# Bulk loads of 16 rows in two buffers in place of 14 rows in three, with the last scaling on GpSimd

## The chip, the core and the metric

The kernel runs on one core of one Trainium2 chip. SyncE issues the transfers and 16 DMA engines carry them; VectorE, ScalarE and GpSimd compute. A load has landed when the last of its 16 engines has reported. The metric is the device time of one execution in microseconds (us). Times given here are medians of several executions on the same chip; the profile describes one execution, and its span (first to last instruction) is about 1.5 us shorter than the device time. The program uses one core, so the "slow" state of a run means only that the run was more than 1.5% above the fastest of the same kernel; the granted clock was 1.0 in all runs.

## The reference

```python
x = np.random.randn(32, 512, 1024).astype(np.float32)
out = (np.sum(x, axis=-1) / 1024.0).astype(np.float32)      # shape (32, 512)
```

There are 16384 rows of 1024 floats, 67 MB to read and 64 KB to write. A "row" in this document means one row on each of the 128 partitions, 0.52 MB; there are 128 of them.

## The kernel before

The first 112 rows come in bulk loads into rotating buffers. VectorE sums each tile with one instruction; of the last tiles, ScalarE sums some rows with its accumulator. Then come ever smaller loads, so that little work is left when the last bytes land. The last two rows are cut up: `row` between ScalarE and VectorE, and the very last one into `pa`, `pb` and `pc`.

```python
main = [(2, 0)] + [(14, 0)] * 6 + [(14, 4), (12, 5)]      # (rows, rows of them on ScalarE)
last = [(8, 4), (4, 2), (2, 1)]
bulk = ctx.enter_context(tc.tile_pool(name="bulk", bufs=3))
...
for rows, on_act in main:
    t = bulk.tile([P, 14, D], F32, name="t")
    load(t[:, :rows, :], x_main[:, j : j + rows, :])       # one DMA, issued from SyncE
    sums(res[:, j : j + rows], t, rows, on_act)            # reduce_sum on VectorE, act_sum on ScalarE
    j += rows
...
c = 768                                                    # row: VectorE sums 768, ScalarE 256
a, b = 448, 704                                            # pa 448 (ScalarE), pb 256 (VectorE), pc 320
...
nc.gpsimd.tensor_scalar_mul(out=res, in0=res, scalar1=scale)
# store of res
act_sum(pc[:, D - b : D - b + 1], pa)
nc.vector.reduce_sum(out=pc[:, D - b + 1 :], in_=pb, axis=AX)
nc.vector.scalar_tensor_tensor(out=fin[:, : L - 1], in0=q[:, : L - 1], scalar=scale,
                               in1=r[:, : L - 1], op0=MULT, op1=ADD)
nc.vector.tensor_scalar(out=scaled, in0=pc, scalar1=scale, scalar2=0.0,
                        op0=MULT, op1=ADD, accum_out=fin[:, L - 1 :])
# store of fin
```

Each partition of a bulk load is one contiguous piece (one descriptor) of 14 * 4 = 56 KB. The load of a tile waits until the tile that had its buffer before has been summed.

## Time and profile before

| | before |
|---|---|
| device time, median | 161.5 us (161.36 to 161.53) |
| span of the profiled run | 159.8 us |
| DMA packets, share of 16 engines' span | 98.0% |
| VectorE busy | 76% |
| landings of 14-row loads | 16.94 us apart |
| VectorE's sum of 14 rows | 15.09 us |
| VectorE idle before each bulk tile | 1.85 us |

The landing distance is the pace of the transfers. The idle time of VectorE before a tile is also a lead: when VectorE frees a buffer, the load in flight lands that much later.

### The profile page before, as it was taken

To read this page: it belongs to the slowest core of one execution; us is meant where nothing else is said; L and a number is where in the kernel's file an instruction comes from. 1 tells how busy PE (TensorE), PEld (TensorE's weight loads), DVE (VectorE), ACT (ScalarE), POOL (GpSimd) and SP (SyncE) were. 2 spreads that over 40 slices of the span, in tenths; PEclk is the share of its full clock that TensorE was granted. 3 is DMA by queue.
4 is the path that set the end of the run, shared out by engine and by line. 5 is a ranking of instruction groups with operands and counts; after the bars stand their busy time and mean duration, and the time that the engine had idled before them with its cause. 6 is when DMAs were issued, how large, how long until landed. Compare 5 with 4: busy or idle time off the path is not lost.

```text
span 159.8 us, 139 instructions
## 1 busy us (share of the span) xinstructions
DVE 121.1 (76%) x17; ACT 19.6 (12%) x37; POOL 0.8 (0%) x6
## 2 busy tenths in 40 slices
DVE  0500059995999599978999599959995996494985
ACT  3000000000000000000000000000001900480973
POOL 0000000000000000000000000000000000001000
DMA  7999999978999999978999999978999999899993
GB/s 250 472 459 459 459 459 459 459 330 359 459 459 459 459 459 459 459 316 373 459 459 459 459 459 459 416 345 388 459 459 427 394 480 505 353 435 390 408 400 132
DMA packets 2592, 67.18 MB, mean 420 GB/s; under 512 B 544, under 2 KB 928, under 8 KB 1056
## 3 DMA queue, kind: packets, MB, share of 16 engines
q1 hardware_dynamic: 2592, 67.18, 98.0%
HBM read 67.11 MB, written 0.07 MB: 420 GB/s over the span
## 4 chain that ended last, share of the span: by engine, by line
DMA 76%; DVE 22%; SPq 1%; issue 0%; DVEq 0%
DMA t<-in_x_dram 56%; DMA row<-in_x_dram 21%; DVE res L153 20%; SPq L142 1%; DVE q L176 1%; DVE scaled L198 0%; DVE pc L193 0%; DVE fin L194 0%; DVEq L198 0%; DVEq L232 0%
## 5 line engine op out<-in xcount | busy, mean ns | idle before, releaser
L153 DVE TENSOR_REDUCE res<-t 128x14 f32<-128x14336 f32 (+3 forms) x9 | 111.2, 12360 | 34.3 <-DMA t<-in_x_dram 34.3
L147 ACT ACTIVATE junk<-t 128x1024 f32<-128x1024 f32 x16 | 16.2, 1013 | 135.9 <-DMA t<-in_x_dram 135.9
L153 DVE TENSOR_REDUCE q<-t 128x4 f32<-128x4096 f32 (+2 forms) x3 | 7.9, 2642 | 2.7 <-DMA t<-in_x_dram 2.5
L147 ACT ACTIVATION_READ_ACCUMULATOR junk<-t 128x1 f32 x16 | 3.0, 187 | 0.0
L147 ACT ACT_TABLE_LOAD x1 | 1.3, 1283 | 1.7 <-PEq L218 1.7
L189 POOL TENSOR_SCALAR res<-res 128x112 f32<-128x112 f32 x1 | 0.5, 494 | 143.8 <-DVE res L153 143.8
L176 DVE TENSOR_REDUCE q<-row 128x1 f32<-128x768 f32 x1 | 1.0, 953 | 0.0
L198 DVE TENSOR_SCALAR_CACHE_REDUCE scaled<-pc 128x322 f32<-128x322 f32 x1 | 0.5, 490 | 0.1
L147 ACT ACTIVATE junk<-pa 128x448 f32<-128x448 f32 x1 | 0.5, 548 | 0.0
L193 DVE TENSOR_REDUCE pc<-pb 128x1 f32<-128x256 f32 x1 | 0.4, 414 | 0.0
L147 ACT ACTIVATE junk<-row 128x256 f32<-128x256 f32 x1 | 0.4, 388 | 0.1
L194 DVE SCALAR_TENSOR_TENSOR fin<-q,r 128x15 f32<-128x15 f32 x1 | 0.2, 176 | 0.0
L147 ACT ACTIVATION_READ_ACCUMULATOR junk<-pa 128x1 f32 x1 | 0.2, 186 | 0.0
L147 ACT ACTIVATION_READ_ACCUMULATOR junk<-row 128x1 f32 x1 | 0.2, 185 | 0.0
L139 POOL MEMSET r<- 128x16 f32 x1 | 0.1, 112 | 1.3 <-POOLq L218 1.3
L218 POOL MEMSET const-bfloat16-1.0<- 128x1 bf16 x1 | 0.1, 103 | 0.0
L218 POOL MEMSET const-uint8-127<- 128x1 uint8 x1 | 0.1, 102 | 0.0
L218 POOL MEMSET const-float32-0.0<- 128x1 f32 x1 | 0.1, 99 | 0.2 <-issue 0.2
L218 POOL MEMSET const-float32-1.0<- 128x1 f32 x1 | 0.1, 99 | 0.0
L198 DVE DVE_READ_ACCUMULATOR scaled<-pc 128x1 f32 x1 | 0.1, 83 | 0.0
## 6 DMA issues: line engine op xcount, KB each, us to landing
t<-in_x_dram SPq DMA_DIRECT2D x7, 7168.0 KB, 35.7
t<-in_x_dram SPq DMA_DIRECT2D x1, 6144.0 KB, 33.3
t<-in_x_dram SPq DMA_DIRECT2D x1, 4096.0 KB, 26.1
t<-in_x_dram SPq DMA_DIRECT2D x2, 1024.0 KB, 18.6
t<-in_x_dram SPq DMA_DIRECT2D x1, 2048.0 KB, 30.5
row<-in_x_dram SPq DMA_DIRECT2D x1, 512.0 KB, 33.2
pa<-in_x_dram SPq DMA_DIRECT2D x1, 224.0 KB, 33.3
pc<-in_x_dram SPq DMA_DIRECT2D x1, 160.0 KB, 33.1
```

The source lines that it names most:

```text
L139: nc.gpsimd.memset(r, 0.0)
L142: tc.keep_in_program_order(nc.sync.dma_start(out=dst, in_=src))
L147: nc.scalar.activation(junk[:, :n], src, COPY, scale=by, accum_out=dst)
L153: nc.vector.reduce_sum(out=dst[:, :d], in_=t[:, :d, :], axis=AX)
L176: nc.vector.reduce_sum(out=q[:, j : j + 1], in_=row[:, :c], axis=AX)
L189: nc.gpsimd.tensor_scalar_mul(out=res, in0=res, scalar1=scale)
L193: nc.vector.reduce_sum(out=pc[:, D - b + 1 :], in_=pb, axis=AX)
L194: nc.vector.scalar_tensor_tensor(out=fin[:, : L - 1], in0=q[:, : L - 1], scalar=scale, in1=r[:, : L - 1], op0=MULT, op1=ADD)
L198: nc.vector.tensor_scalar(out=scaled, in0=pc, scalar1=scale, scalar2=0.0, op0=MULT, op1=ADD, accum_out=fin[:, L - 1 :])
L218: nc = _bacc.Bacc("TRN2", target_bir_lowering=False, num_devices=1)
```

## The change

The intent is fewer and larger loads (64 KB a descriptor, one load fewer), and a shorter tail: the scaling of the last results leaves VectorE for GpSimd, and the splits of the last rows are set anew. To make room, two bulk buffers replace three, and the small tiles get memory of their own.

```diff
-    main = [(2, 0)] + [(14, 0)] * 6 + [(14, 4), (12, 5)]
+    main = [(2, 0)] + [(16, 0)] * 5 + [(16, 2), (14, 6)]
-    bulk = ctx.enter_context(tc.tile_pool(name="bulk", bufs=3))
+    bulk = ctx.enter_context(tc.tile_pool(name="bulk", bufs=2))
-    r = one.tile([P, L], F32, name="r")
-    nc.gpsimd.memset(r, 0.0)
+    r = one.tile([P, 1], F32, name="r")
-        t = bulk.tile([P, 14, D], F32, name="t")
+        if rows > 2:
+            t = bulk.tile([P, 16, D], F32, name="t")
+        else:
+            t = one.tile([P, rows, D], F32, name="t0")
 ... the 8-row tile of the tail moves from bulk to one ...
-    c = 768
+    c = 688
-    a, b = 448, 704
+    a, b = 480, 672
-    nc.vector.scalar_tensor_tensor(
-        out=fin[:, : L - 1], in0=q[:, : L - 1], scalar=scale, in1=r[:, : L - 1], op0=MULT, op1=ADD
+    nc.gpsimd.tensor_scalar_mul(out=fin[:, :j], in0=q[:, :j], scalar1=scale)
+    nc.gpsimd.tensor_scalar(
+        out=fin[:, j : j + 1], in0=q[:, j : j + 1], scalar1=scale, scalar2=r, op0=MULT, op1=ADD
     )
```

More of the change, by code (lines that the diff above doesn't have):

```diff
@@ L162 @@
     for rows, on_act in last:
-        if rows == 8:
-            t = bulk.tile([P, 14, D], F32, name="t")[:, :8, :]
-        else:
-            t = one.tile([P, rows, D], F32, name=f"t{rows}")
+        t = one.tile([P, rows, D], F32, name=f"t{rows}")
         load(t, x_last[:, j : j + rows, :])
@@ L169 @@
         j += rows
-    c = 768
+    c = 688
     row = one.tile([P, D], F32, name="row")
     load(row, x_last[:, j, :])
-    act_sum(r[:, j : j + 1], row[:, c:], by=scale)
+    act_sum(r, row[:, c:], by=scale)
     nc.vector.reduce_sum(out=q[:, j : j + 1], in_=row[:, :c], axis=AX)
-    a, b = 448, 704
+    a, b = 480, 672
     pa = one.tile([P, a], F32, name="pa")
```

## The prediction

> **What bounds the kernel now.** The kernel sums 16384 rows of 1024 floats, 128 rows (0.52 MB) per "row step" of the 128 partitions, and moves 67.18 MB. I read the page's totals first, then the order of time, then short windows over the start, then the last microseconds.
>
> ```profile
> span 159.8 us, 139 instructions
> DVE 121.1 (76%) x17; ACT 19.6 (12%) x37; POOL 0.8 (0%) x6
> ...
> q1 hardware_dynamic: 2592, 67.18, 98.0%
> ```
>
> The packets of the one DMA queue fill 98% of the 16 engines' span; VectorE is busy for 76% only. The chain of waits agrees in kind (DMA 76%, DVE 22%), but its DVE share is misleading: where it walks through a 15.1 us reduction it follows the release of a buffer, and two other loads were in flight at that time. The order of time shows it:
>
> ```profile
> 38.71 15.09 DVE L153 TENSOR_REDUCE res<-t 128x14 f32<-128x14336 f32 x1 [1.87 <-DMA t<-in_x_dram]
> 55.65 15.09 DVE L153 TENSOR_REDUCE res<-t 128x14 f32<-128x14336 f32 x1 [1.84 <-DMA t<-in_x_dram]
> 72.59 15.09 DVE L153 TENSOR_REDUCE res<-t 128x14 f32<-128x14336 f32 x1 [1.86 <-DMA t<-in_x_dram]
> ...
> 123.41 10.82 DVE L153 TENSOR_REDUCE res<-t 128x10 f32<-128x10240 f32 x1 [1.85 <-DMA t<-in_x_dram]
> 137.94 7.62 DVE L153 TENSOR_REDUCE res<-t 128x7 f32<-128x7168 f32 x1 [3.72 <-DMA t<-in_x_dram]
> 147.66 4.42 DVE L153 TENSOR_REDUCE q<-t 128x4 f32<-128x4096 f32 x1 [2.09 <-DMA t<-in_x_dram]
> ```
>
> Columns: start, duration, engine, instruction, then how long the engine sat idle and for whom. Each bulk reduction starts when its load lands, and landings are 16.94 us apart (14 rows), then 14.53 (12 rows, 123.41 to 137.94) and 9.72 (8 rows). That is 1.21 us a row step whatever the load's size: 7.34 MB in 16.94 us is 433 GB/s. From 14 and 12 rows, a row step costs (16.94-14.53)/2 = 1.205 us, and what is left over is 16.94-14*1.205 = 0.07 us per load. So loads carry almost no fixed cost while the queue is full. VectorE finishes each tile 1.85 us before the next lands.
>
> The end, in the order of time:
>
> ```profile
> 156.18 0.39 ACT L147 ACTIVATE junk<-row 128x256 f32<-128x256 f32 x1
> 156.18 0.95 DVE L176 TENSOR_REDUCE q<-row 128x1 f32<-128x768 f32 x1
> 156.72 0.55 ACT L147 ACTIVATE junk<-pa 128x448 f32<-128x448 f32 x1
> 157.17 0.18 DVE L194 SCALAR_TENSOR_TENSOR fin<-q,r 128x15 f32<-128x15 f32 x1
> 157.20 0.19 ACT L147 ACTIVATION_READ_ACCUMULATOR junk<-pa 128x1 f32 x1
> 157.26 0.41 DVE L193 TENSOR_REDUCE pc<-pb 128x1 f32<-128x256 f32 x1
> 157.79 0.49 DVE L198 TENSOR_SCALAR_CACHE_REDUCE scaled<-pc 128x322 f32<-128x322 f32 x1
> 158.31 0.34 SPq L201 DMA_DIRECT2D out_dram<-fin  x1
> ...
> pc<-in_x_dram SPq DMA_DIRECT2D x1, 160.0 KB, 33.1
> ```
>
> The last piece pc is issued at 124.39 and lands 33.1 us later, at 157.49. Its sum starts at 157.79, 0.11 us after VectorE is done with pb at 157.68. So at the very end VectorE, not the transfer, sets the time, by 0.2 to 0.25 us. That is all that the end can give.
>
> **What the Trainium skill says.** "DMA: Bandwidth & Descriptors", section "Where 436 GB/s comes from": the SBUF ports pass 435.2 GB/s. The trace agrees: 433 GB/s between landings. So there is nothing left for larger descriptors to win in mid-stream. The same page, "Latency and other measured facts", puts the first byte of a load issued from SyncE at about 0.6 us; here the first packets start 1.0 us or more after the issue (windows below), so I use the trace. "VectorE: DVE Perf Modes", the perf-mode tier table: tensor_reduce runs in the 1x mode alone. The trace agrees: 14336 elements at 0.96 per ns are 14.93 us of the 15.09. "GPSIMD Engine Reference", section 4.1: one-input elementwise work is roughly line rate there; in the trace the scaling of 112 columns took 0.494 us on GpSimd, started 0.09 us after the last reduction and released the store 0.03 us after its end.
>
> **The change, part by part.** The instruction order of both kernels shows no new wait on any path but this: with two bulk buffers, loads 3 to 7 (counted from 0, the 2-row load) wait each for the reduction of the load two before. The 8-row load and all after it have their own memory.
>
> (a) *One bulk load fewer before the tail*, 8 in place of 9 for the same 112 rows: 0.07 us less, by the working above.
>
> (b) *Buffers.* Before, a load waited for the reduction three back, so it was issued about 1.85+16.94 = 18.8 us before the queue would run dry. A 16-row reduction takes, by the line through the 14-row (15.09) and 10-row (10.82) ones, 1.067 us a row plus 0.15, so 17.22 us. A 16-row load lands 16*1.205+0.07 = 19.35 us after the one before. So load k+2 is issued 19.35-17.22-0.04 = 2.09 us before load k+1 lands, with nothing else queued. Is that enough? The start of the kernel shows a load on an empty queue:
>
> ```profile
> 0.00:1.00 1.00, 0.00 (x0) 0.00 (x0) 0.19 (x4) 1.00 0.00 0
> 1.00:1.25 0.25, 0.00 (x0) 0.00 (x0) 0.00 (x0) 1.00 2.85 393
> ...
> 4.00:4.50 0.50, 0.00 (x0) 0.00 (x0) 0.00 (x0) 1.00 4.48 1933
> ```
>
> The last two columns are the DMA share and GB/s, and packets seem to be counted where they start (shares over 1). The issue at 0.00 gives first packets at 1.0 to 1.25 us; the next load's 56 KB packets start at 4.0 to 4.5, so the first load's data end there, and VectorE sees the landing at 4.83, some 0.35 later. A refill must thus arrive 1.1+0.35 = 1.45 us before the landing of the load in flight; it has 2.09. It is hidden with 0.6 us to spare, if the latency of its first read also fits into that. I take the cost as 0, with the rival below.
>
> (c) *The tail's arithmetic.* VectorE's reductions follow 0.153 us + 1.042 ns an element (768: 0.953, 256: 0.414). From the landing of row, taken at 156.11 after (a): 688 elements 0.87, to 156.98; no SCALAR_TENSOR_TENSOR (0.18 and its gap removed); pb, 192 elements, 0.35, to about 157.37. ScalarE: 336 elements 0.455 (slope 0.83 ns from 256 and 448), plus the 0.15 gap that the trace has before pa, so pa starts at 156.72; 480 elements 0.575, and the accumulator read ends 0.12 later, at 157.42. pc lands at 157.42. All three meet within 0.05 us, which is what the new splits were chosen for. Add 0.11 for the hand-over: the last sum starts at 157.55 in place of 157.79. It is 32 elements longer (0.034), so the store leaves 0.24-0.03 = 0.21 us earlier. This includes the 0.07 of (a).
>
> (d) *GpSimd* now scales the 15 columns in two operations, the second waiting for row's two sums (157.0). With 0.09 to start and less than the 0.494 of the 112-column one it is done by 157.6, before the last sum ends at 158.1. Off the path. The memset that is gone ran at 1.73 us, beside the first load: worth nothing.
>
> Sum: 161.5 - 0.2 - 0 = 161.3 us.
>
> **The rivals.** (1) *Two buffers leave the queue dry.* For it: the whole first load took 4.83 us, of which 1 MB at 433 GB/s explains 2.42; the other 2.41 us exceed the lead of 2.09 by 0.32. A stall delays the next landing and gives the following refill as much more lead, so only loads 3, 5 and 7 would pay: 3*0.32 = 1 us, 162.3 us. Against it: that load was the first of all, and a read that arrives while the engines still stream can overlap its latency. The small last store, issued at 158.31, reached its landing in 1.4 us. (2) *Larger descriptors move faster.* If the 0.07 us were larger in truth, or engines were out of step at load ends, 64 KB pieces could win up to 0.5 us: 160.8. Against it: the row step is 1.21 us at every size and the ceiling is 435. (3) *GpSimd comes on the path at the end*: a per-partition scalar operand or a slow start of over 0.7 us would delay the last store by some tenths: 161.6. (4) *VectorE becomes the bound*: 17.22 against 19.35 us per load leaves it slack; the last bulk load gives it 8 rows (8.7 us) against 9.7 until the 8-row load lands, so no.
>
> **Range and chances.** No stall, about two in three: 161.1 to 161.4. A partial or full stall, about one in three: 161.5 to 162.4. A gain of 2% needs 158.3 us, and the bytes alone at 433 GB/s take 155 us plus 2.4 at the start and 2.3 at the end: out of reach. A loss of 2% needs 3.2 us, more than a full stall at all five refills (1.6). I predict 161.3 us, 160.9 to 162.4.
>
> **What would show it.** Right: bulk reductions of about 17.22 us, 19.3 to 19.4 us apart, idle 2.1 us before each; last sum about 0.24 us earlier; GpSimd done before it. Wrong: landings alternating, 19.65 and 19.35 or so, mean a dry queue, by the excess; even landings below 19.2 mean that descriptor size counts; a last store that waits for GpSimd means (d) failed.

## The result and the profile after

The changed kernel takes 167.53 us (167.24, 167.26, 167.81 and one slow run of 169.76) against 161.5. The ratio of the fast runs is 1.037, with an interval of 1.034 to 1.040: slower, and far outside the predicted range. Ratios here are the mean time of one kernel's fast runs over that of the other's fast runs of the same rounds, so they are not quite the ratio of the medians.

The totals of the changed kernel's page:

```profile
span 165.7 us, 133 instructions
...
q1 hardware_dynamic: 2448, 67.18, 96.2%
```

The span is 5.9 us longer, and the DMA engines are busy for a smaller share of it: they have waited. But they were also busy for longer with the same bytes: 96.2% of 165.7 us is 159.4 us, and 98.0% of 159.8 was 156.6. So about 2.8 of the 5.9 us are packets that took longer, and about 3.1 us are engines that stood still. The order of time shows where (start, duration, instruction, then VectorE's idle time before it):

```profile
43.67 17.22 DVE L152 TENSOR_REDUCE res<-t 128x16 f32<-128x16384 f32 x1 [2.14 <-DMA t<-in_x_dram]
65.44 17.22 DVE L152 TENSOR_REDUCE res<-t 128x16 f32<-128x16384 f32 x1 [4.55 <-DMA t<-in_x_dram]
84.85 17.22 DVE L152 TENSOR_REDUCE res<-t 128x16 f32<-128x16384 f32 x1 [2.19 <-DMA t<-in_x_dram]
107.12 17.22 DVE L152 TENSOR_REDUCE res<-t 128x16 f32<-128x16384 f32 x1 [5.04 <-DMA t<-in_x_dram]
...
143.74 8.69 DVE L152 TENSOR_REDUCE res<-t 128x8 f32<-128x8192 f32 x1 [2.10 <-DMA t<-in_x_dram]
```

The reductions last 17.22 us, as worked out. The loads do not land evenly: load 3 (counted from 0) lands 21.77 us after load 2, load 4 19.41 after that, load 5 22.27, load 6 19.44 (it lands at 126.56). Against a pace of 19.35, loads 3 and 5 are late by 2.42 and 2.92 us, and load 7 (14 rows, 17.18 against 16.94) by 0.24. That makes 5.6 of the 5.9 us. Every other load is late: a late landing gives the next refill a lead of 4.5 to 5 us, and that one comes in time. The chain of work that ended last walks through the late loads, from issue to landing:

```profile
41.56 23.86 DMA t<-in_x_dram
...
82.69 24.41 DMA t<-in_x_dram
```

The bytes of 16 rows take 19.35 us, so these two loads carry 4.5 and 5.1 us that are not bytes; in the first 2.1 us of them the load before was still landing. What the engines did after the issue at 41.56 is seen in half-microsecond windows of the changed kernel. The last two columns are the DMA share and GB/s, and a packet is counted in the window in which it starts; one 64 KB packet in half a microsecond reads as 131 GB/s:

```profile
42.50:43.00 0.50, 0.00 (x0) 0.00 (x0) 0.00 (x0) 1.00 0.74 262
43.00:43.50 0.50, 0.00 (x0) 0.00 (x0) 0.00 (x0) 1.00 2.38 918
43.50:44.00 0.50, 0.33 (x1) 0.00 (x0) 0.00 (x0) 1.00 0.00 0
44.00:44.50 0.50, 0.50 (x1) 0.00 (x0) 0.00 (x0) 1.00 1.14 393
44.50:45.00 0.50, 0.50 (x1) 0.00 (x0) 0.00 (x0) 1.00 1.48 524
...
45.50:46.00 0.50, 0.50 (x1) 0.00 (x0) 0.00 (x0) 1.00 2.80 918
46.00:46.50 0.50, 0.50 (x1) 0.00 (x0) 0.00 (x0) 1.00 0.78 262
```

Nine packets start by 43.5, one on each of nine engines, and seven only between 44.0 and 45.0. So seven of the 16 engines stood still for about 1.5 us: by the single packets of the trace they started 2.8 to 3.2 us after the issue, at 44.40 to 44.73. Of the nine, six went on without a pause. From the durations (share times 8 us, over the number of packets) the first packets took about 2.8 us (0.74 and 2.38 make 25 us for nine) and 3.0 us (1.14 and 1.48 make 21 us for seven), where an undisturbed one takes 2.42; the second packets of the nine took 3.2 (2.80 and 0.78 make 29 us). After two such slow rounds the packets take 2.42 again. Load 3 is therefore late for two reasons: even its first engine reports 0.9 us late, and the seven that stood still report 1.5 to 1.9 us after that one.

The tail of the changed kernel:

```profile
162.84 0.57 ACT L146 ACTIVATE junk<-pa 128x480 f32<-128x480 f32 x1
163.10 0.35 DVE L192 TENSOR_REDUCE pc<-pb 128x1 f32<-128x192 f32 x1
163.12 0.27 POOL L194 TENSOR_SCALAR fin<-q,r 128x1 f32<-128x1 f32 x1 [0.71 <-DVE q L175]
...
163.70 0.52 DVE L198 TENSOR_SCALAR_CACHE_REDUCE scaled<-pc 128x354 f32<-128x354 f32 x1 [0.25 <-ACT junk L146]
```

The last sum now waits for ScalarE, not for VectorE's own earlier work, and pc itself landed at the same time (163.53, and ScalarE was done at 163.54); GpSimd is done 0.3 us before the last sum starts. From the start of VectorE's sum of `row` (162.14; 156.18 before) to the last store (164.26; 158.31 before) it is 2.12 us, against 2.13 before. The tail neither gains nor loses.

### The profile page after: what moved, and what is told of

Same layout as the page of the kernel before. It is cut to its first block, busy times and chain, and to the rows that moved or that the text cites. A ratio compares the mean times of both kernels' runs of the same rounds, so it can differ in the third digit from the quotient of the medians.

```text
span 165.7 us, 133 instructions
## 1 busy us (share of the span) xinstructions
DVE 121.8 (74%) x15; ACT 18.7 (11%) x35; POOL 1.2 (1%) x7
## 3 DMA queue, kind: packets, MB, share of 16 engines
q1 hardware_dynamic: 2448, 67.18, 96.2%
## 4 chain that ended last, share of the span: by engine, by line
DMA 65%; DVE 32%; SPq 2%; ACT 0%; issue 0%; ACTq 0%; DVEq 0%
DMA t<-in_x_dram 44%; DVE res L152 31%; DMA pa<-in_x_dram 22%; SPq L141 2%; ACT junk L146 0%; DVE scaled L198 0%; ACTq L232 0%; DVEq L198 0%; DVEq L232 0%
## 5 line engine op out<-in xcount | busy, mean ns | idle before, releaser
L152 DVE TENSOR_REDUCE res<-t 128x16 f32<-128x16384 f32 (+3 forms) x8 | 112.2, 14019 | 40.3 <-DMA t<-in_x_dram 40.3
L146 ACT ACTIVATE junk<-t 128x1024 f32<-128x1024 f32 x15 | 15.2, 1013 | 142.8 <-DMA t<-in_x_dram 142.8
L175 DVE TENSOR_REDUCE q<-row 128x1 f32<-128x688 f32 x1 | 0.9, 870 | 0.1
L198 DVE TENSOR_SCALAR_CACHE_REDUCE scaled<-pc 128x354 f32<-128x354 f32 x1 | 0.5, 523 | 0.2 <-ACT junk L146 0.2
L146 ACT ACTIVATE junk<-pa 128x480 f32<-128x480 f32 x1 | 0.6, 574 | 0.1
L146 ACT ACTIVATE junk<-row 128x336 f32<-128x336 f32 x1 | 0.5, 454 | 0.2 <-DMA row<-in_x_dram 0.2
## 6 DMA issues: line engine op xcount, KB each, us to landing
t<-in_x_dram SPq DMA_DIRECT2D x1, 7168.0 KB, 19.4
```

The costliest lines, as they stand in the source:

```text
L146: nc.scalar.activation(junk[:, :n], src, COPY, scale=by, accum_out=dst)
L152: nc.vector.reduce_sum(out=dst[:, :d], in_=t[:, :d, :], axis=AX)
L175: nc.vector.reduce_sum(out=q[:, j : j + 1], in_=row[:, :c], axis=AX)
```

## The experiments

"Lead" below is the time from the issue of a refill to the landing of the load then in flight, as the trace of each run has it at its first refill. The first theory, A, was that with two buffers the queue runs dry. Runs e1 to e4 shared one chip and the same runs of the kernel before, so did e5 to e8, and e9 to e11; e12 ran alone.

### e1: the tail alone

The changed kernel with the loads, tiles and buffers of the kernel before:

```diff
-    main = [(2, 0)] + [(16, 0)] * 5 + [(16, 2), (14, 6)]
+    main = [(2, 0)] + [(14, 0)] * 6 + [(14, 4), (12, 5)]
-    bulk = ctx.enter_context(tc.tile_pool(name="bulk", bufs=2))
+    bulk = ctx.enter_context(tc.tile_pool(name="bulk", bufs=3))
 ... tiles of 14 rows; the 2-row and the 8-row tile in bulk again ...
```

> The loads, tiles and three buffers of the kernel before, with the new tail alone (splits 688, 480 and 192, the scaling of fin on GpSimd). Theory A (the two buffers leave the queue dry): the tail is innocent, 161.2 to 161.6 us; from row's landing to the last store about as long as before (2.1 us). Rival T (GpSimd or the new splits in the tail cost): 162 us or more.

Measured: 161.42 us against 161.21, ratio 1.001 (0.999 to 1.003). From the landing of `row` to the last store it is 2.1 us again. The tail is innocent, and it gains nothing either.

### e2: the loads alone

The kernel before with the new `main`, two buffers of 16 rows and the small tiles in memory of their own; the old tail.

```diff
-    main = [(2, 0)] + [(14, 0)] * 6 + [(14, 4), (12, 5)]
+    main = [(2, 0)] + [(16, 0)] * 5 + [(16, 2), (14, 6)]
-    bulk = ctx.enter_context(tc.tile_pool(name="bulk", bufs=3))
+    bulk = ctx.enter_context(tc.tile_pool(name="bulk", bufs=2))
 ... tiles of 16 rows; small tiles in one ...
```

> The new loads (16 rows, two buffers, small tiles of their own) with the old tail. Theory A: the whole loss, 166.8 to 168 us, landings again about 21.8 and 22.3 us apart at loads 3 and 5. Rival T: below 165 us.

Measured: 166.99 us, ratio 1.034 (1.029 to 1.039). Loads 3 and 5 landed 22.25 and 22.05 us after the one before. The loads carry the whole loss.

### e3: two buffers, with 14 rows

```diff
-    bulk = ctx.enter_context(tc.tile_pool(name="bulk", bufs=3))
+    bulk = ctx.enter_context(tc.tile_pool(name="bulk", bufs=2))
 ... kernel before; small tiles in one ...
```

> The kernel before, 14-row loads, with two bulk buffers in place of three and the small tiles in memory of their own: one thing changed that matters, the buffers. The refill is issued about 1.85 us before the load in flight lands. Theory A: loads 3, 5 and 7 land 2 to 3 us late each, in sum 6 to 8 us, 167 to 169 us. Rival D (descriptors of 64 KB are what stalls, whatever the buffers): within 0.5 us of the kernel before, 161.3 to 162.

Measured: 170.03 us, ratio 1.046 (1.043 to 1.048). Two of the four runs count as slow; the fast ones, 168.42 and 168.93, give the ratio and lie in the range of theory A. The order of time of this run, two late loads:

```profile
57.07 15.09 DVE L153 TENSOR_REDUCE res<-t 128x14 f32<-128x14336 f32 x1 [3.37 <-DMA t<-in_x_dram]
...
94.24 15.09 DVE L153 TENSOR_REDUCE res<-t 128x14 f32<-128x14336 f32 x1 [5.10 <-DMA t<-in_x_dram]
```

With 56 KB descriptors the idle time before VectorE grows from 1.85 to 3.4 and 5.1 us at loads 3 and 5. So 64 KB descriptors are not needed for the stall (rival D falls); the missing third buffer is enough.

### e4: VectorE frees the buffers sooner, lead 6.4 us

```diff
-    main = [(2, 0)] + [(16, 0)] * 5 + [(16, 2), (14, 6)]
+    main = [(2, 0)] + [(16, 4)] * 5 + [(16, 4), (14, 6)]
```

> The changed kernel (16 rows, 64 KB descriptors, two buffers) with 4 rows of each bulk tile summed on ScalarE, so that VectorE frees the buffer after 12.95 us in place of 17.22 and the refill is issued about 6.4 us before the landing in place of 2.1. Theory A: all stalls gone, landings 19.36 us apart throughout, 161.3 to 161.7 us. Rival D: landings still late at every other load, 166 us or more.

Measured: 161.68 us against 161.21, ratio 1.002 (1.0005 to 1.0035). All 16-row loads landed 19.34 to 19.36 us apart. Two buffers and 64 KB descriptors are harmless if the buffer is freed early enough. ScalarE, idle in this stage before, does the extra work beside VectorE.

### e5 and e6: leads of 3.2 and 4.2 us

As e4, with `(16, 1)` and with `(16, 2)` in place of `(16, 4)`; the last 16-row tile has `(16, 2)` in both.

> The changed kernel with 1 row of each 16-row tile on ScalarE: VectorE frees the buffer after 16.15 us, and the refill is issued about 3.2 us before the landing in place of 2.1. Theory A with a threshold (what counts is whether the refill's descriptors reach each of the 16 engines before it runs dry, and the trace of the changed kernel shows restarts 1.0 to 3.5 us after the issue and engines 0.4 to 0.8 us apart): nearly all of the loss gone, 161.6 to 162.8 us. Rival G (the loss falls off in proportion to the missing lead, from 5.8 us at 2.1 to about 0 at 6.4): about 165.5 us.

Measured: 163.97 us (163.0 to 164.56), ratio 1.016 (1.011 to 1.020), which the 2% rule calls unclear; the interval still lies clear of 1. This misses both forecasts: more loss than a clean threshold, less than a proportional one. The order of time of this run shows why:

```profile
62.89 16.15 DVE L152 TENSOR_REDUCE res<-t 128x15 f32<-128x15360 f32 x1 [3.19 <-DMA t<-in_x_dram]
83.17 16.15 DVE L152 TENSOR_REDUCE res<-t 128x15 f32<-128x15360 f32 x1 [4.13 <-DMA t<-in_x_dram]
```

Load 3, refilled with a lead of 3.2 us, landed in time (19.35 us after load 2). Load 4, refilled with the same lead, landed 0.93 us late, and load 6 1.99 us late. At a lead of 3.2 us the same refill sometimes holds and sometimes not.

> As the last with 2 rows of each bulk tile on ScalarE, lead about 4.2 us. Theory A with a threshold: no loss, 161.5 to 161.8 us. Rival G: about 164 us.

Measured: 161.5 us against 161.29, ratio 1.001 (0.9997 to 1.0027). At 4.2 us of lead nothing is lost; a bulk tile of this run reads

```profile
63.03 15.09 DVE L152 TENSOR_REDUCE res<-t 128x14 f32<-128x14336 f32 x1 [4.27 <-DMA t<-in_x_dram]
```

### e7: half the descriptor at the same lead

```diff
-        load(t[:, :rows, :], x_main[:, j : j + rows, :])
+        if rows > 2:
+            h = rows // 2
+            load(t[:, :h, :], x_main[:, j : j + h, :])
+            load(t[:, h:rows, :], x_main[:, j + h : j + rows, :])
+        else:
+            load(t[:, :rows, :], x_main[:, j : j + rows, :])
```

> The changed kernel, two buffers of 16 rows and VectorE alone, but each bulk tile is loaded by two transfers of 8 rows (descriptors of 32 KB), so the lead stays about 2.1 us and the descriptor halves. Theory A1 (the stall is the time to restart a dry engine): loss about the same, 165.5 to 168 us. Rival A2 (the stall is one descriptor's time, since an engine that comes late is one whole descriptor late): about half the loss, 163.5 to 165 us.

Measured: 167.89 us (166.51 to 168.13), ratio 1.042 (1.040 to 1.043). Halving the descriptor does not halve the loss. In the profiled run, the fastest of the five, load 3 was 1.2 us late, again about the time of one packet (1.21 us for 32 KB), but load 5 was 2.9 us late as in the changed kernel. So the length of a packet does not set the whole loss; whether it sets that of load 3 is not shown.

### e8: the same memory in four buffers of 8 rows

```diff
-    main = [(2, 0)] + [(16, 0)] * 5 + [(16, 2), (14, 6)]
+    main = [(2, 0)] + [(8, 0)] * 12 + [(8, 2), (6, 3)]
-    bulk = ctx.enter_context(tc.tile_pool(name="bulk", bufs=2))
+    bulk = ctx.enter_context(tc.tile_pool(name="bulk", bufs=4))
 ... tiles of 8 rows ...
```

> The same 128 KB of bulk memory per partition as four buffers of 8 rows in place of two of 16, VectorE alone, the new tail. A refill is issued about 20 us before the queue would run dry. Theory A: no stall; 14 bulk loads in place of 7, at 0.07 us each, 161.5 to 162.2 us. Rival M (it is the smaller bulk memory, 128 KB in place of 168, that costs): 166 us or more.

Measured: 161.98 us against 161.29, ratio 1.004 (1.003 to 1.006); bulk tiles landed 9.7 us apart. The bulk memory is 128 KB a partition as in the changed kernel, and VectorE does all the work as there, but up to three loads stand in the queue. It is not the amount of memory that costs, but how few pieces it is cut into. Against e6 the 14 bulk loads in place of 7 cost 161.98 - 161.5 = 0.48 us, 0.07 us a load, just the fixed cost that the prediction had read from the landings.

### e9: the restart by itself

One bulk buffer, deliberately slow: every bulk load from the second on meets an empty queue.

```diff
-    bulk = ctx.enter_context(tc.tile_pool(name="bulk", bufs=2))
+    bulk = ctx.enter_context(tc.tile_pool(name="bulk", bufs=1))
```

> One bulk buffer of 16 rows, on purpose slow: each load is issued when its tile has been summed, 17.2 us after the last landing, so the queue is empty and every engine idle at each issue. This measures the restart by itself: from issue to landing, less 19.35 us of bytes. Theory R1 (a restart costs what the first load of the kernel paid, 2.4 us): 21.8 us from issue to landing, about 277 us in all. Theory R2 (a refill always costs what loads 3 and 5 of the changed kernel paid from issue to landing, 23.9 and 24.4 us, so 4.5 to 5 us): about 290 us in all.

Measured in one look: 277.55 us. The chain of work of this run has the loads from issue to landing, for instance

```profile
41.44 21.70 DMA t<-in_x_dram
```

The five refills of 16 rows took 21.68 to 21.80 us. With 19.35 us of bytes, a restart from an empty queue costs 2.3 to 2.45 us, like the first load of the kernel. The windows after this issue show what the restart is made of:

```profile
42.00:42.50 0.50, 0.00 (x0) 0.00 (x0) 0.00 (x0) 1.00 2.44 786
42.50:43.00 0.50, 0.00 (x0) 0.00 (x0) 0.00 (x0) 1.00 3.46 1180
43.00:43.50 0.50, 0.00 (x0) 0.00 (x0) 0.00 (x0) 1.00 0.31 131
```

The 16 engines start one after another (the first 0.96 us after each of the five issues, the last 1.4 to 1.8), and the first packet of each takes 3.1 us in place of 2.42 (6.21 times 8 us over 16). The state of a single run is unknown; these are times within one profile. So the 4.5 and 5.1 us of the changed kernel are not the price of a restart as such.

### e10 and e11: refills that come later still

On purpose, VectorE sums the first row (e10) or the first two rows (e11) of each bulk tile a second time into a spare column, which holds the buffer longer. The leads are about 1.0 us and -0.1 us.

```diff
+        if rows > 2:
+            nc.vector.reduce_sum(out=again, in_=t[:, :1, :], axis=AX)      # e11: t[:, :2, :]
         sums(res[:, j : j + rows], t, rows, on_act)
```

> The changed kernel with the first row of each bulk tile summed a second time into a spare column, on purpose: VectorE holds each buffer 1.22 us longer, and the refill is issued about 0.87 us before the landing in place of 2.1, when the faster engines are already dry. Theory R1 (fixed restart of 2.4 us from an idle queue; what the changed kernel paid on top comes from refills that arrive just as the engines run dry and scatter them): load 3 lands 1.6 us late or little more, 21 us after load 2. Theory R2 (restart of 4.5 to 5 us): load 3 lands about 3.6 us late, in sum 169 to 172 us.

Measured: 165.95 us (165.57 to 166.02), ratio 1.027 (1.026 to 1.029). More work for VectorE and a later refill, yet a faster kernel than the changed one. The chain of work of this run has the first refill as

```profile
42.62 21.80 DMA t<-in_x_dram
```

It is issued 1.06 us later than in the changed kernel and lands at 64.42 in place of 65.42, though load 2 had landed at the same time to within 0.1 us. The windows after its issue:

```profile
43.50:44.00 0.50, 0.41 (x1) 0.00 (x0) 0.00 (x0) 1.00 3.11 1049
44.00:44.50 0.50, 0.50 (x1) 0.00 (x0) 0.00 (x0) 1.00 2.27 918
44.50:45.00 0.50, 0.50 (x2) 0.00 (x0) 0.00 (x0) 1.00 0.30 131
```

All 16 engines start within about a microsecond, one group of 8 + 7 + 1, and not in two groups. By the packets of the trace only this first round is slow (2.8 us), where the changed kernel has two.

> The same with two rows summed again, 2.29 us: the refill is issued 0.2 us after the landing, when all engines have been dry for about half a microsecond. Theory R1: load 3 lands 2.6 us late, about 22 us after load 2, all engines together (spread as at the start). Theory R2: 4.7 us late, 24 us after load 2.

Measured: 168.94 us (168.88 to 169.13), ratio 1.047 (1.045 to 1.048). Load 3 took 21.81 us from issue to landing and landed 21.93 us after load 2, 2.6 late, as the fixed restart has it. Loads 5 and 7 were late by 2.7 and 2.6 us. These three restarts, 7.8 us, cover all that the kernel lost (168.94 - 161.44 = 7.5 us), although VectorE, now at 19.4 us a tile, has no slack left against 19.35.

### e12: between the two

The same with half a row summed again (`t[:, :1, :512]`), lead about 1.5 us.

> The changed kernel with half a row of each bulk tile summed again, 0.69 us: the refill is issued about 1.4 us before the landing, between the 2.1 of the changed kernel (load 3 late by 2.4 us, engines scattered) and the 0.87 of the run with a whole row (late by 1.5 us, engines together). Theory R1 with scatter (a refill that reaches the engines after all are dry pays 2.45 us less the lead; one that reaches them while some still run scatters them): descriptors that take 1.0 us from the issue come when most engines are dry, so load 3 lands 1.0 to 1.3 us late and the whole takes 164.3 to 165.5 us, less than at either lead. If the scatter already reaches down to 1.4 us of lead: 166.5 us or more.

Measured: 167.93 us, from 165.93 to 168.5; two of the four runs count as slow. The fast runs are 165.93, as fast as e10, and 167.43, the profiled one. The forecast of 164.3 to 165.5 us failed. The profiled run had load 3 late by 1.36 us, just above the 1.0 to 1.3 expected, but load 5 by 2.1 and load 7 by 3.0. The reason is in the engines. Every load counts up its semaphore in 16 steps, one for each engine, and the trace has the times; first and last engine of each load in us:

```text
load   changed kernel     e10 (lead 1.0)     e12 (lead 1.5)
  2    43.26 -  43.65     43.10 -  43.57     42.97 -  43.26
  3    63.53 -  65.42     63.84 -  64.43     63.17 -  63.97
  4    83.24 -  84.83     83.26 -  83.75     82.52 -  83.30
  5   104.41 - 107.10    104.19 - 104.79    103.07 - 104.77
  6   123.81 - 126.54    123.53 - 124.14    122.56 - 124.13
  7   143.33 - 143.72    142.09 - 142.65    141.52 - 144.07
```

In e10 the engines stay within 0.6 us of each other. In the changed kernel and in e12 they drift apart with the refills, up to 2.7 us, and a landing counts the last engine. At load 6 the first engine of the changed kernel is no later than 0.3 us behind that of e10; the last is 2.4 us behind. Engines once apart keep their distance through a load that comes in time (load 4 after 3, load 6 after 5), so the next refill again finds some of them still at work and others dry. It is also why load 7 of the changed kernel was late by only 0.24 us: when it was issued, at 124.36, fourteen engines were done with load 6 and two were to run until 126.5; the fourteen paid for their restart beside the work of those two, which load 6 had waited for anyway.

### The runs by lead

| run | lead of the first refill | time | before in the same rounds | ratio |
|---|---|---|---|---|
| kernel before (three buffers) | about 19 us | 161.5 | | |
| e4 | 6.4 us | 161.68 | 161.21 | 1.002 |
| e6 | 4.2 us | 161.5 | 161.29 | 1.001 |
| e5 | 3.2 us | 163.97 | 161.29 | 1.016 |
| changed kernel | 2.1 us | 167.53 | 161.5 | 1.037 |
| e7 (half descriptors) | 2.1 us | 167.89 | 161.29 | 1.042 |
| e3 (14 rows) | 1.8 us | 170.03 (fast runs 168.42, 168.93) | 161.21 | 1.046 |
| e12 | 1.5 us | 167.93 (fast runs 165.93, 167.43) | 161.37 | none |
| e10 | 1.0 us | 165.95 | 161.44 | 1.027 |
| e11 | -0.1 us | 168.94 | 161.44 | 1.047 |

The lead alone does not decide a refill. Over all the refills of these runs, a lead of 3.6 us or more cost 0.4 us at most. A lead of 2.2 us or less left loads 3 and 5 late by 1.2 us or more in every run. Between the two it went both ways: with 2.5 to 3.3 us all seven refills of e3, e7, e10, e11 and e12 landed in time, each behind a load that was itself late, while two of the three with 3.2 us in e5 did not.

No version beat both kernels: e6, the best with 64 KB descriptors, equals the kernel before.

## Why the prediction was wrong

It forecast no change and the kernel lost 3.7%. By its steps:

- **What bounds the kernel** was right: transfers at 1.21 us a row, at any size. Undisturbed 16-row loads landed 19.35 us apart, and rival 2 (larger descriptors move faster) fell with that.
- **Step (a), one load fewer**, 0.07 us, had the right size (e8 against e6), but is far below what was lost.
- **Step (b), buffers, is the step that failed.** Its working of the lead (2.09 us; 2.1 to 2.2 in the trace) and of the reduction (17.22 us) was exact. The sentence "A refill must thus arrive 1.1+0.35 = 1.45 us before the landing of the load in flight; it has 2.09" was wrong. It took the first engine's start (1.1 us after the issue) for the end of the restart and left the rest to "if the latency of its first read also fits". It did not: in the changed kernel seven engines got their first packet of load 3 only 2.8 to 3.2 us after the issue. A restart from empty costs 2.3 to 2.45 us (e9), which is what the very first load shows if one takes the whole of it (4.83 - 2.42); by e9 that also holds the later starts of other engines and the slower first packets. Beyond that, the landing that counts is the last engine's, while the first engine runs dry 0.3 to 0.7 us sooner. Behind an undisturbed load, a lead of 3.2 us was not always enough and one of 4.2 us was (e5, e6).
- **Rival 1** named the mechanism and its signature: loads 3, 5 and 7 late, the others in time. The term of its sum that was mis-sized is the stall, "3*0.32 = 1 us". It subtracted the lead from the restart as if a refill on a half-dry queue paid only the rest. That holds when the refill finds all engines dry (e10: issued 0.95 us before the last engine of load 2 landed, load 3 late by 1.5 us, and 2.45 - 0.95 is 1.5). It does not hold at a lead of 2.1 us: the refill reached some engines still running and others just stopped, seven of 16 restarted about 1.5 us behind the rest, two rounds of packets were slow, and loads 3 and 5 were 2.42 and 2.92 us late. From this error also came the claim that all five refills together could cost 1.6 us at most.
- **Step (c), the tail**, forecast 0.14 us beside step (a) and got nothing. It let ScalarE start on `pa` 0.61 us after `row`, with a gap that it took for ScalarE's own. In truth ScalarE waits there for the landing of `pa`: in the trace before, the 16 engines' increments for `pa` end at 156.70 and ScalarE starts at 156.72. A larger `pa` lands later still, and ScalarE started 0.70 us after `row`. VectorE's saved instruction was worth nothing because ScalarE took its place at the end, together with pc, which landed 1.41 us after row in place of 1.34.
- **Step (d), GpSimd**, was right: 0.26 and 0.27 us, off the path.

That the loss comes from the loads, from two buffers and from the lead is shown by e2, e3, e4 and e6. That a refill 1.1 us later can cost less is shown by e10 against the changed kernel (ratios 1.027 and 1.037, intervals apart), and the traces show the difference in two places: engines that drift apart, and a second slow round of packets. Why an engine that runs dry while others are still served restarts later than all engines together do, and why the first packets after such a refill last longer, stays open: no run separates the issuing side from the memory side.

## What to carry to other kernels

With two buffers, the lead of a refill is the load's time less the time that the buffer is held. Compare that with the whole restart of an idle queue (issue to landing less the bytes, read off the first load), plus the distance between the engines, and stay well above the sum (here it is 2.8 us; a lead of 3.2 was not enough, one of 4.2 was, and nothing between was tried); if it falls short, cut the same memory into more, smaller buffers or let an idle engine shorten the hold, before trying larger transfers. A transfer-bound kernel with an almost balanced consumer has little idle time to show, and that same small number is its entire margin once the third buffer is gone.

## What the Trainium skill lacked or had wrong

- "DMA: Bandwidth & Descriptors", section "Anatomy of one DMA — SWDGE (gpsimd) path", gives a fixed cost of about 2.0 us a transfer for DMAs issued from GpSimd. It does not say what a queue that runs dry costs when SyncE issues. Here a restart from empty took 2.3 to 2.45 us (e9), with first packets of 3.1 us in place of 2.42, and a refill issued 2.1 us before the queue ran dry still landed 2.4 and 2.9 us late (changed kernel).
- The same page, "Latency and other measured facts", puts the first byte at about 0.6 us and does not say from where it counts. On an empty queue the first packet started 0.96 us after the start of the issuing instruction (e9), which itself took 0.33 us: 0.63 us after its end, in agreement with the page if it counts from there. What it lacks is the last of the 16 engines, which started 1.4 to 1.8 us after the issue.
- No page tells that engines which ran dry at different moments stay apart for the following loads. Here they were up to 2.7 us apart in the changed kernel.
- "Trainium Kernel Development and Optimization", section "Best Practices", advises double-buffering to overlap DMA with compute. It does not say how far ahead a refill must be issued: here two buffers with 2.1 us of lead lost 3.7%, with 4.2 us nothing.
- "GPSIMD Engine Reference" has no fixed cost for a small one-input operation: here one column took 0.265 us and 14 columns 0.261, against 0.493 for 112.
